# A gated MLP's projection down as Strassen's seven products over pairs of tiles, on one Trainium2 core

## The chip, the cores and the metric

The kernel runs on one core of one Trainium2 chip. The core has a matrix engine (PE, TensorE), a vector engine (DVE), an activation engine (ACT), a general engine (POOL, GpSimd) and a sequencer that mostly issues transfers (SP). Each engine works through its own list of instructions strictly in that list's order, and waits on semaphores where it needs another engine's result. Times are device microseconds (us) of one execution.

## The reference, cut to what matters

One layer of a decoder over 1024 tokens of width 1024: three groups of attention heads, an output projection, a gated MLP of width 2816, a gated per-layer embedding and a last norm. All of it is float32.

```
r  = x + mix @ w_out                                  # 1024 x 1024 @ 1024 x 1024
h2 = rmsnorm(r, ffn_norm)
g  = causal_dwconv3(h2 @ w_gate) + conv_b             # D_FF = 2816
r  = r + (gelu(g) * (h2 @ w_up)) @ w_down             # 2816 -> 1024: the part that is changed
gate = sigmoid(rmsnorm(r, ple_norm) @ w_ple_gate)
r  = r + (p @ w_ple_proj) * gate
return rmsnorm(r, final_norm)
```

## The kernel before, in words

Everything is kept transposed: features on the 128 partitions, tokens along the row. P is 128, T is 1024 (all tokens), H2 is 512 (half of them), KD is 8 tiles of width, NF is 22 tiles of the MLP's width. PE's accumulators are eight PSUM banks of 128 x 512: three under `pg`, five under `b1`.

A float32 product is made of three matmuls (`mm3`, lines 115 to 119): each operand is split by `hl` (line 771) into a rounded part `hi` (a cast on ACT, L772) and the rest `lo` (a subtraction on DVE, L773), and PE adds hi*hi, hi*lo and lo*hi into one bank.

The stages after attention, in program order:

- **Projection out** (`out_tile_half`, line 806): 16 pieces of work, one for each of 8 output tiles and 2 halves of the tokens. Each takes 24 matmuls, its own weights (`wr_wo` from SP's queue, cast to `wh_wo` on ACT, and `wl_wo` by DVE at L106), and ends with the residual's addition on DVE (L813), a write of the half tile to `r_dram` (`rd`) from POOL's queue, and a square on ACT that POOL, or DVE for the last two tiles, adds to `acc2`.
- **Forms and embedding's product** (`form`, `first_halves`): the normed activations and their Strassen combinations are split. The per-layer embedding's product goes to `pp_dram` (`ppd`).
- **Units** (`Unit`, line 907): one for each of the 22 tiles of the MLP's width; it already makes the products with w_gate and w_up by Strassen's seven, 84 matmuls in all, then the convolution and GELU, and multiplies into `us`, which POOL writes to `h3_dram` (line 988). The weights' combinations are made in `weights_up_2`.
- **Projection down**: eight outputs of 128 x 512 at a time, in two passes over f. `h3` comes back from memory, is split again by `h3_parts`, the weights by `weights_down`. The first pass makes output tiles 0 to 3 (both halves), the second tiles 4 to 7, the last seven tiles of f of the second pass output tile by output tile. 8 x 2 x 22 products of three matmuls each. `add_in` adds each to the residual, and `split3` prepares the next product's operand.
- **Embedding's gate** (`embed`): product with w_ple_gate in three pieces of tokens (512, 256, 256), the norm's factor (`rms_bc`), sigmoid, the last norm and the output.

The order on each engine is not the program's order: a scheduler orders all instructions ahead of time by a model of their cost, and `tc.high_priority(offset=...)` moves the instructions in it ahead. A buffer is a slot of a pool under a tag; a tile that takes a slot waits for the last reader of the tile before it. So a tag's number of slots (`BUFS`) sets how far a load may run ahead.

## Time and profile before

| what | us |
|---|---|
| median of 3 runs (lowest to highest) | 1286.43 (1286.18 to 1290.48) |
| the profiled execution, and its span | 1285.93, 1283.7 |
| PE busy, share of the span | 1260.7, 98% |
| DVE, ACT, POOL busy | 815.8 (64%), 537.8 (42%), 103.6 (8%) |
| projection out | about 384 to 450 of the span |
| units 0 to 21 | about 529 to 932 |
| projection down | 932.4 to 1172 |

The profiled execution lies 0.5 us below the median, and 2.2 us of it lie outside the span. The clock granted to PE is full except in the last slice. Windows in the tables of the prediction are in us from the span's start; "L773" is line 773 of the kernel before. In groups of instructions the number behind `x` is their count, then busy time and the mean duration in ns, then the idle time of the engine before them with what ended it.

### The profile page before, as it was taken

Reading aid. Unit: us, or ns where it says so; the run is one execution under the profiler, and the core shown is the slowest. Engines: PE = TensorE matmul, PEld = TensorE weight load, DVE = VectorE, ACT = ScalarE, POOL = GpSimd, SP = SyncE. Lnnn points to the kernel's source line nnn. Section 1 sums busy time; section 2 is a strip of 40 time slices with the busy share of each in tenths; the row PEclk is TensorE's granted clock in tenths of the full one; section 3 lists DMA queues with packets and bytes.
Section 4 is the critical chain, followed back from the end, with each engine's and each line's share of the span. In section 5 each row is a group of like instructions: output and inputs, shape, how many; then the busy total and the mean of one; then the engine's idle time right before and its main releaser. Section 6 shows DMA issues by size and latency. Waiting matters only on the chain.

```text
span 1283.7 us, 16183 instructions
## 1 busy us (share of the span) xinstructions
PE 1260.7 (98%) x6330; PEld 1057.6 (82%) x6330; DVE 815.8 (64%) x1388; ACT 537.8 (42%) x842; POOL 103.6 (8%) x113
## 2 busy tenths in 40 slices
PE   9999999999999999999999999999999999999996
PEld 7888888887888888787888888888888888888896
DVE  7986967567776477976776666666356123346576
ACT  6324233257665256543444344344235123334432
POOL 2000000013111231000000000000000021001010
PEclk9999999999999999999999999999999999999998
DMA  7110110111004745132122222222457215323132
GB/s 250 50 34 17 34 33 18 48 35 34 18 17 143 288 133 197 61 115 99 66 82 99 72 87 88 83 82 77 161 166 262 65 54 200 107 91 115 42 107 82
DMA packets 42236, 122.29 MB, mean 95 GB/s; under 512 B 5168, under 2 KB 7728, under 8 KB 42160
## 3 DMA queue, kind: packets, MB, share of 16 engines
q1 hardware_dynamic: 32032, 89.14, 21.5%
q0 software_dynamic: 8544, 30.41, 6.4%
q10 hardware_dynamic: 1584, 1.71, 0.4%
q8 instruction: 49, 0.80, 0.2%
q14 instruction: 27, 0.22, 0.1%
HBM read 97.13 MB, written 24.12 MB: 94 GB/s over the span
## 4 chain that ended last, share of the span: by engine, by line
PE 68%; issue 11%; DVE 2%; POOL 2%; ACT 1%; DMA 0%; DVEq 0%; POOLq 0%; ACTq 0%
PE d L119 6%; PE d L117 6%; PE d L118 6%; PE gb L119 5%; PE gb L118 5%; PE gb L117 5%; PE gd L117 2%; PE gd L119 2%; PE gd L118 2%; PE pg L118 2%; PE pg L117 2%; PE pg L119 2%; PE o L117 2%; PE o L119 2%; PE o L118 2%
## 5 line engine op out<-in xcount | busy, mean ns | idle before, releaser
L117 PE MATMUL gb<-b,f 128*128 128x512 f32 x176 | 69.1, 393 | 0.2
L118 PE MATMUL gb<-b,f 128*128 128x512 f32 x176 | 68.7, 390 | 0.0
L119 PE MATMUL gb<-b,f 128*128 128x512 f32 x176 | 68.6, 390 | 0.0
L117 PE MATMUL pg<-hp,hpg 128*128 128x256 f32 (+1 forms) x192 | 61.7, 322 | 0.0
L118 PE MATMUL pg<-lp,hpg 128*128 128x256 f32 (+1 forms) x192 | 61.1, 319 | 0.0
L119 PE MATMUL pg<-hp,lpg 128*128 128x256 f32 (+1 forms) x192 | 61.1, 319 | 0.0
L773 DVE TENSOR_TENSOR l<-h3r,h 128x1024 fp32r<-128x1024 f32 x32 | 38.9, 1224 | 34.4 <-ACT h L772 34.2
L976 DVE TENSOR_TENSOR gs<-ga,s 128x512 f32<-128x512 f32 x19 | 13.1, 691 | 68.8 <-PE ga L119 68.8
L772 ACT CAST h<-h3r 128x1024 fp32r<-128x1024 f32 x34 | 35.4, 1050 | 43.2 <-PE d L118 20.2
L988 POOL DMA_DIRECT2D h3d<-us x22 | 11.7, 534 | 415.8 <-DVE us L987 379.9
L781 POOL TENSOR_TENSOR acc<-acc,sq 128x512 f32<-128x512 f32 (+1 forms) x15 | 29.0, 1936 | 166.2 <-ACT sq L780 165.9
L117 PEld LDWEIGHTS gb<-b,f 128*128 128x128 f32 x176 | 33.0, 188 | 8.6 <-ACT gs L939 1.6
L772 ACT CAST f<-s 128x1024 fp32r<-128x1024 f32 x22 | 23.2, 1055 | 38.6 <-PE gb L119 33.7
L119 PEld LDWEIGHTS gb<-b,f 128*128 128x128 f32 x176 | 33.1, 188 | 7.0
L950 ACT ACTIVATE cv<-cv 128x1024 f32<-128x1024 f32 x22 | 23.4, 1061 | 36.7 <-DVE cv L948 36.7
L118 PEld LDWEIGHTS pg<-lp,hpg 128*128 128x128 f32 x192 | 36.6, 191 | 2.6 <-DVE lp L1085 0.2
L119 PEld LDWEIGHTS pg<-hp,lpg 128*128 128x128 f32 x192 | 36.6, 191 | 2.5
L117 PEld LDWEIGHTS pg<-hp,hpg 128*128 128x128 f32 x192 | 36.6, 191 | 2.5
L118 PEld LDWEIGHTS gb<-b,f 128*128 128x128 f32 x176 | 33.1, 188 | 6.7
L772 ACT CAST hf<-s 128x1024 fp32r<-128x1024 f32 x22 | 23.2, 1053 | 31.7 <-PE gd L118 30.5
L119 PE MATMUL gd<-b,f 128*128 128x512 f32 x88 | 34.4, 391 | 1.6 <-DVE f L773 1.6
L773 DVE TENSOR_TENSOR f<-s,f 128x1024 fp32r<-128x1024 f32 x22 | 26.9, 1225 | 14.2 <-ACT f L772 14.2
(781 smaller groups left out, 3942.8 us busy)
## 6 DMA issues: line engine op xcount, KB each, us to landing
wu<-w_gu SPq DMA_DIRECT2D x22, 512.0 KB, 3.5
wg<-w_gu SPq DMA_DIRECT2D x22, 512.0 KB, 3.5
h3d<-us POOLq DMA_DIRECT2D x22, 512.0 KB, 2.9
h3r<-h3d SPq DMA_DIRECT2D x22, 512.0 KB, 3.7
wr_wo<-w_out SPq DMA_DIRECT2D x16, 512.0 KB, 3.6
h3r<-h3d POOLq DMA_DIRECT2D x12, 512.0 KB, 4.0
x<-xT SPq DMA_DIRECT2D x16, 256.0 KB, 5.2
r<-xT SPq DMA_DIRECT2D x16, 256.0 KB, 7.0
```

The costliest lines, as they stand in the source:

```text
L117: TE.matmul(o, wh, xh, start=first, stop=False, skip_group_check=on)
L118: TE.matmul(o, wh, xl, start=False, stop=False, skip_group_check=on)
L119: TE.matmul(o, wl, xh, start=False, stop=last, skip_group_check=on)
L772: S.copy(hi, src)
L773: e.tensor_tensor(out=lo, in0=src, in1=hi.bitcast(F32), op=ALU.subtract)
L781: e.tensor_tensor(out=acc[:, cols], in0=acc[:, cols], in1=sq[:, cols], op=ALU.add)
L950: S.activation(cv, cv, AF.Gelu_apprx_tanh)
L976: V.tensor_tensor(out=g0, in0=bank["a"], in1=s1, op=ALU.add)
L988: G.dma_start(h3_dram[f], us)
```

## The change

`w_down` is taken as 11 pairs of tiles by two blocks of 512 columns: four blocks for each pair. With the activations' two tiles of the pair and two token halves this is a 2 x 2 by 2 x 2 product, made by seven products instead of eight. Each product (1, 2, 6, 5, 7, 3, 4 in this order) runs over all 11 pairs and four output tiles at once: 7 x 11 steps of 4 x 3 matmuls. Four banks ("x") hold a sum that goes on through products 1, 6, 7, 4, four others ("y") product 2, and then 5 and 3. After each product DVE adds the four banks into one half of four residual tiles, 28 additions.

- **The sums of activations.** An even unit writes only half its result (`he_dram`). An odd unit writes its own (`ho_dram`), makes four differences of 128 x 512 on DVE, into `cv` and into the even unit's tile, and writes both (`ta_dram`, `tb_dram`).
- **The sums of weights.** `sums_down(n)`, 22 pieces: POOL's queue loads 512 KB of w_down into the one slot of tag `rs`, DVE makes four sums of 128 x 256 in place, POOL's queue writes 512 KB to `s_dram`. Pieces are put into the program from unit 3 on, one for each unit; nothing but the one slot holds them back.
- **The loads.** `parts(g)` takes two steps at a time: the weights into `wraw` or a slot of `ws`, the activations of four steps into a slot of `hx`, all from SP's queue; then both are split, the activations into `big`.
- **What ends a product.** `done(d, h)` squares a finished half tile of the residual (ACT), adds the square to `acc3` (DVE), and makes the next product's operand (`hp` on ACT, `lp` on DVE). It is called for four tiles after each of the products 2, 7, 3 and 4.
- `weights_up_2` makes its combinations with other operands in place, with as many instructions; tag `ws` has 3 slots instead of 4 and `us` has 2.
- The norm's factor in `embed` is made for the two halves apart.

```diff
+NJ = NF // 2
+DOWN = (1, 2, 6, 5, 7, 3, 4)
...
-    BUFS = {"hx": 6, "r": 8, "gs": 1, "cv": 1, "us": 1, "w4": 1, "w5": 1, "ws": 4}
+    BUFS = {"hx": 6, "r": 8, "gs": 1, "cv": 1, "us": 2, "w4": 1, "w5": 1, "ws": 3}
...
-    h3_dram = [dp.tile([P, T], F32, name=f"h3d{f}") for f in range(NF)]
+    he_dram = [dp.tile([P, H2], F32, name=f"hed{j}") for j in range(NJ)]
+    ho_dram = [dp.tile([P, T], F32, name=f"hod{j}") for j in range(NJ)]
+    ta_dram = [dp.tile([P, T], F32, name=f"tad{j}") for j in range(NJ)]
+    tb_dram = [dp.tile([P, T], F32, name=f"tbd{j}") for j in range(NJ)]
+    s_dram = [dp.tile([4, P, H2], F32, name=f"sd{j}") for j in range(NJ)]
...
-            G.dma_start(h3_dram[f], us)
+            j = f // 2
+            if f % 2 == 0:
+                G.dma_start(he_dram[j], u1)
+                even.append(us)
+                return
+            G.dma_start(ho_dram[j], us)
+            e0, e1 = [even[j][:, half(i)] for i in range(2)]
+            t1, t2 = [cv[:, half(i)] for i in range(2)]
+            minus(t1, e0, e1)
+            minus(t2, u0, t1)
+            G.dma_start(ta_dram[j], cv)
+            minus(e0, u0, e0)
+            minus(e1, u1, t2)
+            G.dma_start(tb_dram[j], even[j])
+    def sums_down(n):
+        j, c = n // 2, slice(n % 2 * 256, n % 2 * 256 + 256)
+        t = cp.tile([P, 4, 256], F32, tag="rs", bufs=1, name=f"sd{n}")
+        G.dma_start(t, a["w_dn"][j][:, :, c].rearrange("b p c -> p b c"))
+        a11, a12, a21, a22 = [t[:, i, :] for i in range(4)]
+        V.tensor_tensor(out=a22, in0=a21, in1=a22, op=ALU.add)
+        minus(a21, a11, a21)
+        minus(a11, a22, a11)
+        minus(a12, a12, a11)
+        G.dma_start(s_dram[j][:, :, c].rearrange("b p c -> p b c"), t)
...
+        sums_down(f - 3)
...
+    for n in range(NF - 3, NF):
+        sums_down(n)
+    steps = [(i, j) for i in DOWN for j in range(NJ)]
+    raws = {}
+    def operands(i, j):
+        w = a["w_dn"][j]
+        x = {1: w[0], 2: w[1], 4: w[3], 6: s_dram[j][0], 3: s_dram[j][1], 7: s_dram[j][2], 5: s_dram[j][3]}[i]
+        y = {1: he_dram[j], 2: ho_dram[j][:, half(1)], 3: ho_dram[j][:, half(0)], 5: ta_dram[j][:, half(0)],
+             6: ta_dram[j][:, half(1)], 7: tb_dram[j][:, half(0)], 4: tb_dram[j][:, half(1)]}[i]
+        return x, y
+    def parts(g):
+        with tc.high_priority(offset=300):
+            if g % 2 == 0:
+                raws[g // 2] = f4("hx", f"hr{g}", (P, 4, H2))
+                for x in range(4 * (g // 2), min(len(steps), 4 * (g // 2) + 4)):
+                    nc.sync.dma_start(raws[g // 2][:, x % 4, :], operands(*steps[x])[1])
+            n = min(2, len(steps) - 2 * g)
+            rw = f4("ws" if g % 2 else "wraw", f"wdr{g}", (P, 2, H2))
+            for x in range(n):
+                nc.sync.dma_start(rw[:, x, :], operands(*steps[2 * g + x])[0])
+            got = []
+            for raw, tags in ((rw, ("whi", "wlo")), (raws[g // 2][:, g % 2 * 2:g % 2 * 2 + 2, :], ("big", "big"))):
+                hi, lo = [f4(t, f"{c}{t}d{g}", (P, 2, H2), F32R) for c, t in zip("hl", tags)]
+                hl(hi[:, :n], lo[:, :n], raw[:, :n])
+                got.append((hi, lo))
+        return got
...
+    def done(d, h):
+        c = half(h)
+        if not acc3:
             acc3.append(f4("ws", "acc3"))
-        sum_squares(acc3[0], r[d], d == 0, tag="ws", e=G if d < KD - 2 else V)
-    def split3(d, tags):
-        hi, lo = [f4(t, f"{c}p{d}", dt=F32R) for t, c in zip(tags, "hl")]
-        for c in [half(0), half(1)] if d == KD - 1 else [slice(0, T)]:
-            S.mul(hi[:, c], r[d][:, c], col(C_G3 + d))
-            V.scalar_tensor_tensor(out=lo[:, c], in0=r[d][:, c], scalar=col(C_G3 + d), in1=hi[:, c].bitcast(F32),
-                                   op0=ALU.mult, op1=ALU.subtract)
-        gs3[d] = (hi, lo)
+        if d == (0 if h else 4):
+            S.square(acc3[0][:, c], r[d][:, c])
+        else:
+            sq = fp.tile([P, H2], F32, tag="s1", bufs=1, name=f"sq{d}{h}")
+            S.square(sq, r[d][:, c])
+            V.tensor_tensor(out=acc3[0][:, c], in0=acc3[0][:, c], in1=sq, op=ALU.add)
+        if d not in gs3:
+            gs3[d] = [f4(t, f"{c}p{d}", dt=F32R) for t, c in zip(TAGS3[d], "hl")]
+        hi, lo = gs3[d]
+        S.mul(hi[:, c], r[d][:, c], col(C_G3 + d))
+        V.scalar_tensor_tensor(out=lo[:, c], in0=r[d][:, c], scalar=col(C_G3 + d), in1=hi[:, c].bitcast(F32),
+                               op0=ALU.mult, op1=ALU.subtract)
...
-        with tc.high_priority(offset=500):
-            raw = f4("ws" if d < 3 or d % 2 else "wraw", f"wpg{d}")
+        with tc.high_priority(offset=300 if d > 2 else 0):
+            raw = f4("us" if d < 3 else "ws" if d % 2 else "wraw", f"wpg{d}")
...
-    for f in range(NF):
-        x = streamed(f, 0) if f < NR else kept(f)
-        h3[f] = x
-        w = weights_down(a["w_dn0"][f], 4, f"a{f}")
-        if f == NF - 4:
-            for i in range(2):
-                residual(i)
+    TO = {1: (0, 1), 6: (0, 0), 7: (4, 0), 4: (4, 1), 2: (0, 1), 5: (4, 0), 3: (0, 0)}
+    DONE = {2: (0, 1), 7: (4, 0), 3: (0, 0), 4: (4, 1)}
+    got = {}
+    bank = {}
+    for n, (i, j) in enumerate(steps):
+        if n % 2 == 0:
+            got[n // 2] = parts(n // 2)
+        if n == 4:
+            for x in range(4):
+                residual(x)
+        (wh, wl), (xh, xl) = got[n // 2]
+        to = "y" if i in (2, 5, 3) else "x"
+        new = i in (1, 2, 5)
+        if new and j == 0:
+            bank[to] = [(pg if (d < 2 if to == "y" else d == 0) else b1)(f"d{i}{d}") for d in range(4)]
         for d in range(4):
-            for h in range(2):
-                down(os[d][h], w, d, x, h, f == 0, f == NF - 1)
-    for d in range(4):
-        add_in(d, os[d])
-    os = banks(1)
-    for n, f in enumerate([*range(NR, NR + NE), *range(NR)]):
-        x = streamed(f, 1) if f < NR else h3[f]
-        w = weights_down(a["w_dn1"][f], 4, f"b{f}")
-        for d in range(4):
-            for h in range(2):
-                down(os[d][h], w, d, x, h, n == 0, False)
-    for d in range(4):
-        split3(d, ("r", "r"))
-    for i in range(2, 4):
-        residual(i)
-    for d in range(4):
-        w = weights_down(a["w_dn2"][d], NK, f"c{d}")
-        for x in (d,) if d < 3 else range(3, KD):
-            gate_weights(x)
-        for h in range(2):
-            for i in range(NK):
-                down(os[d][h], w, i, h3[NR + NE + i], h, False, i == NK - 1)
-        add_in(4 + d, os[d])
-        split3(4 + d, (("gs", "cv"), ("us", "w4"), ("w5", "ws"), ("big", "big"))[d])
+            mm3(bank[to][d], wh[:, n % 2, d * P:d * P + P], wl[:, n % 2, d * P:d * P + P], xh[:, n % 2, :],
+                xl[:, n % 2, :], new and j == 0, j == NJ - 1, not new)
+        if j == NJ - 1:
+            d0, h = TO[i]
+            for d in range(4):
+                V.tensor_tensor(out=r[d0 + d][:, half(h)], in0=bank[to][d], in1=r[d0 + d][:, half(h)], op=ALU.add)
+            if i in DONE:
+                d0, h = DONE[i]
+                for d in range(4):
+                    done(d0 + d, h)
+            if i in (2, 6, 5):
+                gate_weights((2, 6, 5).index(i))
+    for d in range(3, KD):
+        gate_weights(d)
...
-                rms_bc(acc3[0], rs3, slice(0, T), "p")
+                rms_bc(acc3[0], rs3, half(0), "p0")
                 acc4.append(f4("ws", "acc4"))
+            if n == 0 and d == 4:
+                rms_bc(acc3[0], rs3, half(1), "p1")
```

The changed kernel's lines 115 to 117 are `mm3`'s matmuls, 770 and 771 `hl`, 104 the `wl_wo` subtraction, 817 the addition in the projection out, 818 its write `rd`, 1009 and 1015 the load and the write of `sums_down`, 1011 and 878 its sums, 1111 to 1120 `done`, 1156 the additions to the residual.

How the instructions stand on three places. First, DVE in the projection out, before: `wl_wo30` is the `lo` part of the weights for output tile 3, half 0; `r3` the addition of tile 3.

```order
L106 TENSOR_TENSOR wl_wo40_3701<-wr_wo40_3697,wh_wo40_3699 128x1024
L813 TENSOR_TENSOR r2_3545<-o20_3630,r2_3545 128x512
L813 TENSOR_TENSOR r3_3546<-o30_3667,r3_3546 128x512
L106 TENSOR_TENSOR wl_wo50_3738<-wr_wo50_3734,wh_wo50_3736 128x1024
L813 TENSOR_TENSOR r4_3547<-o40_3704,r4_3547 128x512
L106 TENSOR_TENSOR wl_wo60_3775<-wr_wo60_3771,wh_wo60_3773 128x1024
L813 TENSOR_TENSOR r5_3548<-o50_3741,r5_3548 128x512
L106 TENSOR_TENSOR wl_wo70_3812<-wr_wo70_3808,wh_wo70_3810 128x1024
```

The same stretch of DVE in the change; `sd2` is the slot with piece 2 of the weights' sums.

```order
L104 TENSOR_TENSOR wl_wo40_3734<-wr_wo40_3730,wh_wo40_3732 128x1024
L1011 TENSOR_TENSOR sd2_5185<-sd2_5185 128x256
L878 TENSOR_TENSOR sd2_5185<-sd2_5185 128x256
L817 TENSOR_TENSOR r2_3578<-o20_3663,r2_3578 128x512
L878 TENSOR_TENSOR sd2_5185<-sd2_5185 128x256 x2
L817 TENSOR_TENSOR r3_3579<-o30_3700,r3_3579 128x512
L104 TENSOR_TENSOR wl_wo50_3771<-wr_wo50_3767,wh_wo50_3769 128x1024
L817 TENSOR_TENSOR r4_3580<-o40_3737,r4_3580 128x512
L1011 TENSOR_TENSOR sd3_5325<-sd3_5325 128x256
L104 TENSOR_TENSOR wl_wo60_3808<-wr_wo60_3804,wh_wo60_3806 128x1024
L878 TENSOR_TENSOR sd3_5325<-sd3_5325 128x256 x3
```

Pieces 0 to 5 stand on DVE between the weights' splits of the projection out, from piece 2 on one for every two output tiles, and pieces 6 and 7 among its last tiles; POOL's list has each piece's load and write between the `rd` writes and the additions to `acc2`. From unit 0 to unit 8 the other pieces follow, three for every two units.

Second, ACT where product 2 ends and product 6 begins, in the change. PE goes from product 2's last matmul straight to one that reads `hwhid11`, the `hi` weights of group 11 (two steps, the first two of product 6); the fourth matmul reads their `lo`, which DVE makes from it. `rr0` and `rr1` are residual tiles, `hpg1` a part of w_ple_gate.

```order
L1111 ACTIVATE acc3_7958<-rr0_7610 128x512
L1119 ACTIVATE hp0_7960<-rr0_7610,small_68 128x512
L1114 ACTIVATE sq11_7964<-rr0_7610 128x512
L1119 ACTIVATE hp1_7967<-rr0_7610,small_68 128x512
L770 CAST hpg1_8210<-wpg1_8208 128x1024
L1119 ACTIVATE hp2_7974<-rr1_7613,small_68 128x512
L770 CAST hwhid11_7994<-wdr11_7991 128x1024
```

The cast of the weights for the next product stands behind six instructions of `done` and `gate_weights`, the first of which needs product 2's first finished bank.

Third, ACT where product 7 ends and product 3 begins. Group 28, whose activations are `hbigd28`, begins with product 3's second step, 12 matmuls after product 7's last; its third matmul reads the `lo` part of those activations.

```order
L770 CAST hwhid28_8688<-wdr28_8685 128x1024
L1111 ACTIVATE acc3_7958<-rr2_7616 128x512
L1119 ACTIVATE hp4_8643<-rr2_7616,small_68 128x512
L1114 ACTIVATE sq50_8647<-rr2_7616 128x512
L1119 ACTIVATE hp5_8650<-rr2_7616,small_68 128x512
L1119 ACTIVATE hp6_8657<-rr3_7619,small_68 128x512
L1119 ACTIVATE hp7_8664<-rr3_7619,small_68 128x512
L770 CAST hwhid29_8723<-wdr29_8720 128x1024
L1114 ACTIVATE sq60_8654<-rr3_7619 128x512
L770 CAST hbigd28_8692<-hr28_8680 128x1024
```

Here it is the activations' cast that stands behind `done` of product 7.

More of the change, by code (lines that the diff above doesn't have):

```diff
@@ L1046, in down @@
-    def down(o, w, i, x, h, first, last):
-        mm3(o, w[0][:, i, :], w[1][:, i, :], x[0][:, half(h)], x[1][:, half(h)], first, last)
-    def streamed(f, again):
-        return h3_parts(f, again, *[f4("r", f"{c}3{f}{again}", dt=F32R) for c in "hl"])
-    def kept(f):
-        if f == NF - 1 or f == NF - 2:
-            t = f4("hx", f"h3{f}", (P, 2, T), F32R)
-            return h3_parts(f, 0, t[:, 0], t[:, 1])
-        return h3_parts(f, 0, *[f4("big", f"{c}3{f}", dt=F32R) for c in "hl"])
@@ L1058, in banks @@
-    def banks(p):
-        return [[(pg if d * 2 + h < 3 else b1)(f"d{p}{d}{h}") for h in range(2)] for d in range(4)]
+    for n in range(NF - 3, NF):
[8 more added lines that the diff above has]
+        return x, y
```

48 lines of the change are left out of this document (12 added, 36 removed).

## The prediction

> **What bounds the kernel now.** First the page: how full each engine is, slice by slice, and the chain that ended last.
>
> ```profile
> PE 1260.7 (98%) x6330; PEld 1057.6 (82%) x6330; DVE 815.8 (64%) x1388; ACT 537.8 (42%) x842; POOL 103.6 (8%) x113
> DVE  7986967567776477976776666666356123346576
> PE 68%; issue 11%; DVE 2%; POOL 2%; ACT 1%; DMA 0%; DVEq 0%; POOLq 0%; ACTq 0%
> ```
>
> PE is full from end to end and is the chain. So a matmul taken away is worth its place in PE's stream, as long as nothing new makes PE wait. Where DVE is at eight or nine tenths, added DVE work has little room. Second, busy time by stage (the windows of the trace; PE's count is that of its matmuls).
>
> ```profile
> core 0: us, PE busy (x) PEld busy (x) DVE busy (x) ACT busy (x) POOL busy (x), PEclk, DMA share, GB/s
> ...
> 404.00:436.00 32.00, 32.00 (x143) 26.30 (x142) 13.68 (x15) 11.12 (x14) 11.70 (x12) 1.00 0.93 350
> ...
> 529.00:568.00 39.00, 37.07 (x160) 29.27 (x159) 32.82 (x42) 19.35 (x22) 0.97 (x2) 1.00 0.31 104
> 604.00:924.00 320.00, 319.47 (x1407) 263.70 (x1407) 204.31 (x244) 130.04 (x152) 9.05 (x17) 1.00 0.27 90
> 932.40:1172.00 239.60, 239.60 (x1056) 197.74 (x1055) 98.66 (x103) 77.32 (x91) 19.24 (x18) 1.00 0.42 134
> ```
>
> The last row is the projection down: PE busy for all of 239.60 us with 1056 matmuls, 239.60 / 1056 = 0.227 us for each. DVE is at 98.66 / 239.60 = 41% there and the transfers at 134 GB/s; nothing but PE's count sets that stage. The first row is the stage that matters for the added transfers: the DMA engines are 93% busy through the middle of the projection out, at 350 GB/s.
>
> **The matmuls that go.** 16 output halves x 22 tiles x 3 = 1056 become 7 products x 11 pairs x 4 outputs x 3 = 924, of the same shape. 132 x 0.227 = **-29.9 us**. The stage keeps pace otherwise: a group of two steps is 24 matmuls, 5.44 us, and needs two casts and two subtractions of 128x1024.
>
> ```profile
> L773 DVE TENSOR_TENSOR l<-h3r,h 128x1024 fp32r<-128x1024 f32 x32 | 38.9, 1224 | 34.4 <-ACT h L772 34.2
> L772 ACT CAST h<-h3r 128x1024 fp32r<-128x1024 f32 x34 | 35.4, 1050 | 43.2 <-PE d L118 20.2
> ...
> L1076 DVE TENSOR_TENSOR rr<-d,rr 128x512 f32<-128x512 f32 x16 | 10.6, 687 | 11.3 <-PE d L119 11.3
> L1155 ACT ACTIVATE rr<-rr,small 128x512 f32<-128x512 f32 x8 | 5.8, 724 | 2.4 <-DVE pt L1153 2.2
> L780 ACT ACTIVATE sq<-rr 128x512 f32<-128x512 f32 x6 | 3.8, 629 | 7.5 <-DVE rr L1149 7.5
> ```
>
> That is 2.1 us of ACT and 2.4 us of DVE in 5.44, and 1 MB of loads, 193 GB/s against the 350 just seen. With two `whi` slots the cast waits for the group before last to end and is done about 2.5 us later (cast, then subtraction, with hand-overs), 2.9 us early. This cover holds in the middle of a product.
>
> **Two boundaries where it doesn't.** ACT's list puts the work of `done` ahead of the cast that the next product needs. Count from the end of product 2's last matmul. Its first bank is complete nine matmuls earlier, at -2.0; DVE adds it in 0.69, from -1.8 with the hand-over to -1.1. Then ACT does, in order, a square (0.63), a scaled copy (0.72), a square, a scaled copy, the cast of a gate weight (1.05) and a scaled copy: 0.63 + 0.72 + 0.63 + 0.72 + 1.05 + 0.72 = 4.5, to +3.4. Only then comes the cast of group 11's weights, to +4.4, and DVE's `lo` part, to +5.6 or 5.7. PE starts at +4.4, has three matmuls (0.7), and waits again until 5.7: a stall of **5.0 us**. Where product 7 ends, ACT has one square, then 0.72 + 0.63 + 3 x 0.72, the weights' cast 1.05, another square, and then the activations' cast: -1.1 + 0.63 + 0.72 + 0.63 + 2.16 + 1.05 + 0.63 + 1.05 = +5.8, and DVE's `lo` at +7.3 behind a norm addition and `lp7`. PE has the second half of a group to do until 2.72, and two matmuls of the next: 7.3 - 2.72 - 0.45 = **4.2 us**. Sum 9.2, from 7 (hand-overs shorter) to 11. The other three changes of product have the next operands cast ahead in the lists: 0.
>
> **The sums of weights in the projection out.** A piece is load, four DVE sums, write, and then the next load into the one slot: a closed loop. DVE waits for each load in its list, with the weights' splits for PE behind it; whoever is late makes `wl_wo` late, and PE waits for that. The list gives a loop two output tiles, 2 x 24 x 0.227 = 10.9 us. The loop's parts, from the nearest rows (transfers with KB each and us from issue to landing; the first `rd` row is of the window 404 to 436, the second of 450 to 560):
>
> ```profile
> rd<-r POOLq DMA_DIRECT2D x7, 256.0 KB, 5.7
> ...
> ppd<-pst POOLq DMA_DIRECT2D x8, 512.0 KB, 4.4
> ...
> rd<-r POOLq DMA_DIRECT2D x7, 256.0 KB, 2.3
> ...
> ppt<-ppd POOLq DMA_DIRECT2D x4, 512.0 KB, 4.1
> ...
> L620 DVE TENSOR_TENSOR pT<-tb,tmask 128x256 f32<-128x256 f32 x3 | 1.3, 421 | 2.0 <-ACT pT L619 2.0
> ```
>
> Without other load: 4 x 0.42 = 1.7, write 4.4, load 4.1, hand-overs 0.5: 10.7, just the room there is. Between 404 and 436 the same write of 256 KB takes 5.7 instead of 2.3, 3.4 more. With 3.4 more on each transfer the loop is 17.5, 6.6 more than its room. DVE has some room of its own there:
>
> ```profile
> 422.58 0.69 DVE L813 TENSOR_TENSOR r<-o,r 128x512 f32<-128x512 f32 x1 [3.31 <-PE o L119]
> 428.02 0.69 DVE L813 TENSOR_TENSOR r<-o,r 128x512 f32<-128x512 f32 x1 [3.31 <-PE o L119]
> ```
>
> It idles 3.3 us for each tile. So the first slow loop costs 6.6 - 3.3 = 3.3, the next, with the cover gone, up to 6.6; the stretch holds two loops of 17.5, and lateness pushes the third out of it. 3.3 + 4.7 (between the covered and the full price, nearer the full, since POOL's list also has additions to `acc2` between write and load) = **8 us**; from 2 (the load stays at 4 us) to 20 (three loops, none covered).
>
> [...]
>
> **The sums beside the units.** A unit is 84 matmuls, 19.04 us. DVE has 204.31 / 320 x 19.04 = 12.2 of it. Three pieces for two units add 2.6 to each, and the four differences of an odd unit:
>
> ```profile
> L874 DVE TENSOR_TENSOR s<-wg,wu 128x512 f32<-128x512 f32 x15 | 10.3, 685 | 0.0
> ```
>
> 4 x 0.69 = 2.7. An odd unit has 17.5 of 19.04: hidden behind PE. The loop has 38.1 / 3 = 12.7 us there, against 10.7. Only at the start is DVE short: 32.82 of 39 between 529 and 568, plus three pieces (5.0) and one set of differences (2.7), 40.5 of 39. **2 us**, from 0 to 14 (three loops at 17.5 instead of 12.7).
>
> **The end.** After product 4 DVE's list has, ahead of the broadcast of the norm's factor for the first half of the tokens, four additions, four norm additions, four `lp` (near 0.75 each), three subtractions of gate weights and twelve small steps, one every 0.2:
>
> ```profile
> 1275.07 0.17 DVE rq_t L142
> 1275.27 0.17 DVE rb_yf L143
> ```
>
> 8 x 0.69 + 4 x 0.75 + 3 x 1.22 + 12 x 0.2 = 14.6, begun at -1.8: 12.8, with hand-overs about 13.5. PE comes to the broadcast after 56 matmuls, at 12.7: **0.8 us**, from 0 to 3.
>
> **Sum.** -29.9 + 9.2 + 8 + 2 + 0.8 = -9.9. The profiled execution took 1285.93 (span 1283.7, 2.2 outside): 1276.0; the median of the runs is 0.5 higher: **1276.5 us**.
>
> **Rivals.**
> - **The sums are hidden everywhere.** The loads land in 4 us although the DMA engines are full, because the rest of that traffic is early loads for later tiles. -29.9 + 9.2 + 0.8: 1266.5. For it: no wait of PE on a transfer between 404 and 436. Against it: the 5.7 us.
> - **The loop eats the gain.** 16 in the projection out and 5 at the start: -29.9 + 9.2 + 16 + 5 + 0.8 = +1.1, 1287.5. For it: DVE can't pass a waiting sum, POOL's additions stand between write and load. Against it: the burst ends at 436.
> - **Slower: the loop sets the pace of the units.** It decides from 12.7 us on: rows of 1 KB, 512 of them, where `ppd` has 256, could make the loop 14, and 13 pieces would lose 1.3 each, 17. With 16 in the projection out: -29.9 + 9.2 + 16 + 17 + 0.8 = +13, 1299.5. Against it: the DMA engines are at 27% in the units, about half with the new traffic.
> - **The clock falls in the stalls.** PE's longest wait is 2.5 us, and only the end shows what follows idle time:
>
> ```profile
> PE rb_f L166 <- DVE rb_yf L143: 2.5, 1, 2.5
> ...
> 1264.00:1270.00 6.00, 6.00 (x53) 6.00 (x52) 3.48 (x9) 2.90 (x8) 0.00 (x0) 1.00 0.00 0
> 1276.00:1283.00 7.00, 1.19 (x4) 0.93 (x4) 2.50 (x5) 0.00 (x0) 0.00 (x0) 0.50 0.45 150
> ...
> 1256.17 0.64 PE rb_f L166 x4
> 1276.16 1.21 PE rb_f L166 x4
> ```
>
> The same four matmuls take 1.21 us instead of 0.64 after some 6 us with PE mostly idle, at half the clock. If PE ran at half clock for as long as it had stood, 5.0 and 4.2 us of stall would cost 4.6 more: 1281. [...] The drop agrees with the trace; how long it lasts no row shows.
>
> **How the numbers follow.** Forecast 0.46 (its own range 1270 to 1283), hidden 0.17, gain eaten 0.20, slower 0.12, clock 0.05. A measurement tells 0.5% from no change: below 1280.0 is faster, above 1292.9 slower. Faster: 0.37 of the forecast, 0.16 of hidden, 0.01 of the clock: 0.54. Slower: 0.11 of the slow rival, 0.04 of the eaten gain, 0.01 of the forecast: 0.16. The rest, 0.30, is the same. The range goes from a little under the hidden case, 1264, into the gap before the slow one, 1294.
>
> **What would show it.** The down stage should be about 209.5 + 9 us, with 924 matmuls and two PE waits of 4 to 5 us, on ACT's weight cast and DVE's activation `lo`. Between 400 and 450 PE should wait for `wl_wo`, with DVE idle ahead of a sum of `sd` until a transfer lands. Odd units should take 19.0 us. I am wrong if PE waits inside a product, if the `sd` transfers take over 6 us in the units, or if PE doesn't wait in the projection out at all.

## The result, and the profile after

The change makes the kernel slower: 1306.49 us (1305.42 to 1310.03) against 1286.31 us (1285.46 to 1290.48), a ratio of 1.0155 with a 95% interval of 1.0126 to 1.0184. The prediction said 1276.5. The profiled execution is the longest of the runs, 1310.03, 3.5 above the median, so its span, 24.6 us longer than that of before, shows about four microseconds more than the runs do. How much of that lies in which stage is not known; in e4 below, whose program is the same up to the projection down, the first row of the table is 18.2 instead of 20.8.

First the page of the changed kernel, with the same rows as before:

```profile
PE 1249.9 (96%) x6198; PEld 1041.7 (80%) x6198; DVE 907.7 (69%) x1567; ACT 553.1 (42%) x860; POOL 128.1 (10%) x162
PE   9999999999999789999999999999999899899996
PEclk9999999999999889999999999999999899899998
```

PE does 132 matmuls less and is yet at 96% of a longer span. Three notches stand in its row, a wide one and two narrow ones, and each has its notch in the row of the granted clock: slices 14 and 15 of the 40 (the projection out), and two near the end (the projection down).

The stages are measured by the start of the last matmul of each. In the names, `h` and `l` stand for `hi` and `lo`: `hwhid` and `lwlod` are the two parts of the weights of the projection down, `hbigd` and `lbigd` those of its activations. These rows list the matmuls of a tile, with their count, duration in ns (lowest, median, highest), and the start of the first and the last of them; the first four are of the kernel before, from four answers of the trace,

```profile
L119 PE MATMUL o<-hc,wl_wo x32: 388/389/390, 402.6 to 483.9; 128*128 128x512 f32 x32
...
L119 PE MATMUL pp<-pT,wl_pp x32: 389/389/476, 484.6 to 508.0; 128*128 128x512 f32 x32
...
L119 PE MATMUL gb<-b,f x176: 387/389/398, 534.6 to 932.2; 128*128 128x512 f32 x176
...
L119 PE MATMUL d<-h,wdc3wlo x14: 389/389/390, 1163.3 to 1172.1; 128*128 128x512 f32 x14
```

and these of the change:

```profile
L117 PE MATMUL o<-hc,wl_wo x32: 388/389/395, 403.1 to 504.7; 128*128 128x512 f32 x32
...
L117 PE MATMUL pp<-pT,wl_pp x32: 389/389/628, 505.4 to 531.4; 128*128 128x512 f32 x32
...
L117 PE MATMUL gb<-b,lf x176: 387/389/628, 563.0 to 972.1; 128*128 128x512 f32 x176
...
L117 PE MATMUL d<-hbigd,lwlod x308: 387/389/642, 972.8 to 1197.1; 128*128 128x512 f32 x154
```

| us | before | change | difference |
|---|---|---|---|
| to the end of the projection out | 483.9 | 504.7 | +20.8 |
| embedding's product | 24.1 | 26.7 | +2.6 |
| units | 424.2 | 440.7 | +16.5 |
| projection down | 239.9 | 225.0 | -14.9 |
| the rest of the span | 111.6 | 111.2 | -0.4 |

The projection down saves half of what its matmuls are worth; the three stages ahead of it, whose matmuls the change doesn't touch, lose 39.9.

What PE waited for in the change (the trace's waits of PE: total, times, longest; a choice of rows, those of the projection down all among them):

```profile
PE o L117 <- DVE wl_wo L104: 8.1, 2, 6.5
PE gb L115 <- DVE us L944: 4.8, 5, 1.9
PE rb_r L164 <- DVE rb_yr L141: 4.7, 1, 4.7
PE d L115 <- ACT hwhid L770: 4.2, 2, 3.6
PE gd L115 <- ACT us L941: 3.4, 2, 1.8
PE d L115 <- ACT hbigd L770: 2.7, 1, 2.7
...
PE d L116 <- DVE lbigd L771: 1.2, 1, 1.2
...
PE d L117 <- DVE lwlod L771: 0.7, 1, 0.7
```

The rows of `d` are the projection down's, 4.2 + 2.7 + 1.2 + 0.7 = 8.8. Not all of it stands at the two boundaries that the prediction names. The timeline has four of the five waits here (start, duration, what ran; in brackets the idle time before, and what ended it):

```profile
989.31 0.50 PE L115 MATMUL d<-hbigd,hwhid 128*128 128x512 f32 x1 [0.52 <-ACT hwhid L770]
...
990.76 0.50 PE L117 MATMUL d<-hbigd,lwlod 128*128 128x512 f32 x1 [0.72 <-DVE lwlod L771]
...
1136.09 1.22 PE L115 MATMUL d<-hbigd,hwhid 128*128 128x512 f32 x2 [2.66 <-ACT hbigd L770]
1138.50 0.79 PE L116 MATMUL d<-lbigd,hwhid 128*128 128x512 f32 x1 [1.19 <-DVE lbigd L771]
```

The last two are where product 7 ends; the wait where product 2 ends, 3.65, is shown under e4. So the boundaries have 3.65 + 2.66 + 1.19 = 7.5, and 1.2 stand inside product 1, soon after the stage begins.

Behind `wl_wo` and `rb_yr` stands DVE in the projection out. Its timeline there:

```profile
419.54 0.42 DVE L1011 TENSOR_TENSOR sd<-sd 128x256 f32<-128x256 f32 x1 [4.51 <-DMA sd<-w_dn]
...
424.60 0.69 DVE L817 TENSOR_TENSOR r<-o,r 128x512 f32<-128x512 f32 x1 [0.29 <-PE o L117]
435.31 0.42 DVE L1011 TENSOR_TENSOR sd<-sd 128x256 f32<-128x256 f32 x1 [10.02 <-DMA sd<-w_dn]
435.65 1.22 DVE L104 TENSOR_TENSOR wl_wo<-wr_wo,wh_wo 128x1024 fp32r<-128x1024 f32 x1
...
451.07 0.43 DVE L1011 TENSOR_TENSOR sd<-sd 128x256 f32<-128x256 f32 x1 [5.22 <-DMA sd<-w_dn]
451.41 1.22 DVE L104 TENSOR_TENSOR wl_wo<-wr_wo,wh_wo 128x1024 fp32r<-128x1024 f32 x1
```

DVE idles 10.02 us until the load of a piece lands, and the next thing in its list, the moment after the first sum, is the weights' split for which PE stands still. From piece to piece it takes 15.8 us (419.54, 435.31, 451.07), where the list has two output tiles, 10.9. The clock falls with these stalls, at 430.06 and 463.98 us, of 6.47 and 4.65 (windows with PE's busy time and count of matmuls in front; the third number from the end is the granted clock):

```profile
432.90:443.10 10.20, 6.18 (x15) 4.83 (x16) 4.48 (x7) 0.63 (x1) 2.60 (x3) 0.50 0.59 200
467.10:473.80 6.70, 4.78 (x15) 4.19 (x16) 6.03 (x17) 2.44 (x4) 3.44 (x4) 0.50 0.84 273
```

### The profile page after: what moved, and what is told of

It is laid out like the page before. It is cut to its first block, busy times and chain, and to the rows that moved or that the text cites. A ratio compares the mean times of both kernels' runs of the same rounds, so it can differ in the third digit from the quotient of the medians.

```text
span 1308.3 us, 16434 instructions
## 1 busy us (share of the span) xinstructions
PE 1249.9 (96%) x6198; PEld 1041.7 (80%) x6198; DVE 907.7 (69%) x1567; ACT 553.1 (42%) x860; POOL 128.1 (10%) x162
## 5 line engine op out<-in xcount | busy, mean ns | idle before, releaser
L115 PE MATMUL d<-hbigd,hwhid 128*128 128x512 f32 x308 | 122.2, 398 | 6.8 <-ACT hwhid L770 4.2
L116 PE MATMUL d<-lbigd,hwhid 128*128 128x512 f32 x308 | 122.1, 397 | 1.2 <-DVE lbigd L771 1.2
L117 PE MATMUL d<-hbigd,lwlod 128*128 128x512 f32 x308 | 121.8, 395 | 0.7 <-DVE lwlod L771 0.7
L771 DVE TENSOR_TENSOR lwlod<-wdr,hwhid 128x1024 fp32r<-128x1024 f32 (+1 forms) x39 | 47.0, 1208 | 70.8 <-ACT hwhid L770 70.7
L115 PE MATMUL gb<-b,hf 128*128 128x512 f32 x176 | 70.2, 399 | 6.5 <-DVE us L944 4.8
L115 PEld LDWEIGHTS d<-hbigd,hwhid 128*128 128x128 f32 x308 | 59.0, 192 | 20.5 <-ACT hwhid L770 5.0
L115 PE MATMUL gd<-b,f 128*128 128x512 f32 x176 | 68.9, 392 | 3.5 <-ACT us L941 3.4
L116 PEld LDWEIGHTS d<-lbigd,hwhid 128*128 128x128 f32 x308 | 59.1, 192 | 14.2 <-DVE lbigd L771 1.9
L117 PEld LDWEIGHTS d<-hbigd,lwlod 128*128 128x128 f32 x308 | 59.1, 192 | 13.7 <-DVE lwlod L771 1.5
L117 PE MATMUL gd<-b,f 128*128 128x512 f32 x176 | 68.3, 390 | 1.5 <-DVE f L771 1.5
L116 PE MATMUL gb<-b,hf 128*128 128x512 f32 x176 | 69.3, 394 | 0.0
L117 PE MATMUL gb<-b,lf 128*128 128x512 f32 x176 | 69.3, 394 | 0.0
L116 PE MATMUL gd<-b,f 128*128 128x512 f32 x176 | 68.5, 389 | 0.0
L770 ACT CAST hbigd<-hr 128x1024 fp32r<-128x1024 f32 (+1 forms) x39 | 40.3, 1038 | 16.3 <-DMA hr<-hod 8.9
```

Source lines behind the costliest of these rows:

```text
L115: TE.matmul(o, wh, xh, start=first, stop=False, skip_group_check=on)
L116: TE.matmul(o, wh, xl, start=False, stop=False, skip_group_check=on)
L117: TE.matmul(o, wl, xh, start=False, stop=last, skip_group_check=on)
L770: S.copy(hi, src)
L771: e.tensor_tensor(out=lo, in0=src, in1=hi.bitcast(F32), op=ALU.subtract)
```

## The experiments

The theory (W in the expectations): DVE, which can't pass an instruction in its list, stands behind the loads of the weights' pieces, and what PE needs stands behind it. Its rivals: DVE has too much to do beside the units (F), and the added transfers themselves slow the others (T). In the table, times of a stage are worked out as above; the expectations reckon the projection out by another of its rows, 1.4 us earlier. Kernels with a single run (e1 to e6, e8, e10, e12, e13) have no interval; the kernel before took 1286.6 to 1288.0 in the sets of runs beside them.

| kernel | time | to the end of the projection out | embedding's product | units | down |
|---|---|---|---|---|---|
| before | 1286.3 | 483.9 | 24.1 | 424.2 | 239.9 |
| the change | 1306.5 | 504.7 | 26.7 | 440.7 | 225.0 |
| e1, no sums of weights | 1273.9 | 485.6 | 24.1 | 427.8 | 223.0 |
| e2, their transfers alone | 1315.7 | 513.0 | 38.2 | 428.9 | 222.7 |
| e3, pieces from unit 3 on | 1289.3 | 484.1 | 24.1 | 446.2 | 221.7 |
| e4, slots given early | 1292.1 | 502.1 | 26.4 | 440.6 | 209.6 |
| e5, e3 with sums on POOL | 1358.4 | 484.1 | 24.1 | 515.0 | 222.2 |
| e6, their DVE work alone | 1273.4 | 484.0 | 24.1 | 428.5 | 222.9 |
| e7, e5 with e4 | 1348.2 | 485.6 | 24.1 | 517.2 | 210.5 |
| e8, e3 with e4 | 1279.7 | 485.7 | 24.2 | 446.9 | 209.4 |
| e9, one piece a unit, e4 | 1279.4 | 486.2 | 24.1 | 432.9 | 223.5 |
| e10, e3 with added writes | 1289.5 | 484.2 | 24.1 | 446.1 | 222.0 |
| e11, e9 spread otherwise | 1278.6 | 485.7 | 24.1 | 446.9 | 209.5 |
| e12, e1 with e4 | 1257.1 | 484.2 | 24.1 | 425.6 | 210.0 |
| e13, e6 with added writes | 1278.3 | 485.7 | 24.1 | 432.1 | 223.1 |
| e14, pieces at the end of units, e4 | 1262.0 | 484.0 | 24.1 | 430.8 | 211.3 |

**e1: the sums of weights left out.** `sums_down` returns at once, and `operands` reads `w[0]` to `w[3]` in place of `s_dram`.

> All weight sums are left out: no piece is loaded, summed or written, and the four products that would read them read blocks of w_down instead (same sizes, other values). The activations' differences stay. In the change's trace the projection out took 20.9 us longer than before (last matmul at 503.4 instead of 482.5), the embedding's product 2.5, the units 16.5, the projection down 225.1 instead of 239.9. Theory W (DVE stands in its list behind a piece's load) and rival T (the added transfers slow the others): the projection out is back at 86 us, the units within 3 us of 421; 1306.5 - 21 - 2.5 - 14 = 1269, between 1264 and 1274. Rival F (DVE is too full in the units, with the activations' differences as a part): the units keep 5 or more, 1274 to 1280.

1273.9. The loss of the projection out goes but for 1.7, and 12.9 of the units' 16.5 belong to the pieces. The time lies where the ranges of W and T and of F meet, and the 3.6 that stays in the units lies between their marks, so e1 doesn't part the theories. The 3.6 stands at the units' start, a wait of 2.4 us on ACT's `whig` among it; in e12, the same kernel up to there, 1.4 stays, with a wait of 1.8: no matmul of its `ga` and `gb` takes over 504 ns, where e1 has some of 628 and a granted clock of 0.97 between 515 and 575. Between 575 and 935 us PE was busy for 359.9 of 360, so the activations' differences cost nothing there.

**e2: the transfers without the sums.**

```diff
-        a11, a12, a21, a22 = [t[:, i, :] for i in range(4)]
-        V.tensor_tensor(out=a22, in0=a21, in1=a22, op=ALU.add)
-        minus(a21, a11, a21)
-        minus(a11, a22, a11)
-        minus(a12, a12, a11)
```

> The loads and writes of all 22 pieces stay, with their one slot; only the four DVE sums of each piece are left out, so DVE never waits for a piece (the values written are the blocks themselves). Theory W and rival F: as without the pieces, 1266 to 1274, though the transfers are the same 22 MB. Rival T (transfers slow the others): near the change, 1296 or more, with the projection out 15 us longer than before.

1315.7, slower than the change: theory W's number is missed by 40 us. But the trace doesn't say T either. These are the waits between 384 and 510, of POOL, and what follows from them:

```profile
POOL sd L1010 <- DMA sd<-w_dn: 46.0, 12, 8.0
POOL sd L1009 <- DMA sd<-sd: 40.3, 11, 5.2
ACT sq L778 <- POOL acc L779: 34.7, 6, 14.5
DVE wl_wo L104 <- ACT wh_wo L102: 20.4, 9, 13.0
```

Without sums the loop runs on POOL alone, whose next load waits for the write and whose next write waits for the load, 86 us of waits. Behind them in POOL's list stand the additions to `acc2`, behind these ACT's squares, behind these the weights' cast. The standing moved from DVE to POOL, and with it the stall. Theory W had to be worded anew: not DVE, but whichever engine has the wait in its list. Units of 428.9 say nothing for or against T here, since the write of the 17th of the 22 pieces is issued at 555.27 us and the units run from 551 to 980.

**e3: no piece before unit 3.**

```diff
+        if f == 3:
+            hold = cp.tile([P, 4, 256], F32, tag="rs", bufs=1, name="hold")
+            V.tensor_copy(out=hold[:, 0, :1], in_=even[1][:, :1])
         sums_down(f - 3)
```

> The one slot is held by a one-column copy of unit 2's result, so no piece starts before unit 3; the pieces then follow between units 3 and 18, nothing else is changed. Theory W: the projection out and the embedding's product lose nothing (-23.4), the units lose by the number of pieces among them, 22 instead of 14, so 16.5 x 22 / 14 = 26 instead of 16.5: 1306.5 - 23.4 + 9.5 = 1293, 1287 to 1297, with DVE waits on the pieces' loads in the units. Rival F: the loss in the units was at their start, where DVE is fullest and where now no piece falls: 1306.5 - 23.4 - 10 = 1273. Rival T: 1290 to 1306, since the same transfers are made elsewhere.

1289.3: the projection out and the embedding's product are back at their old times, and the units lose more, 446.2, with 22 pieces instead of 14 among them. That is (446.2 - 427.8) / 22 = 0.84 us for a piece, in the change (440.7 - 427.8) / 14 = 0.92. Rival F's 1273 is off. T's range begins at 1290, so by the time alone T is hardly excluded.

**e4: the slots of `acc3` and the last operand given early.**

```diff
             for x in range(4):
                 residual(x)
+            acc3.append(f4("ws", "acc3"))
+            gs3[7] = [f4("big", f"{c}p7", dt=F32R) for c in "hl"]
+            for x in (acc3[0], *[y.bitcast(F32) for y in gs3[7]]):
+                G.memset(x[:, :1], 0.0)
```

> acc3 and the last operand's two tiles are given their slots at the fifth step of the projection down, by a one-column memset each; ACT's list then has the next product's casts ahead of the work that ends a product. Theory on the boundaries: the two PE stalls there (4.2 and 0.7 us on the weights, 2.7 and 1.2 on the activations, 8.8 in all) go, and with them the time at a lower clock after each, about 4.6: 1306.5 - 13.4 = 1293, projection down 211 to 213 us. Rival (the clock after a stall costs nothing): 1298, 216 us. Rival (PE only waits elsewhere, later in the product): 1304 or more.

1292.1, the projection down 209.6, less than the 211 to 213 expected; PE has no wait in it at all (a window of the stage; PE's busy time and its count of matmuls follow the length):

```profile
969.30:1179.00 209.70, 209.70 (x926) 173.48 (x926) 125.51 (x133) 92.68 (x105) 3.06 (x5) 1.00 0.64 211
```

209.7 us, with 926 matmuls in the window, is 29.9 below the 239.6 of before. The projection down costs 225.0 - 209.6 = 15.4 more in the profiled run of the change, of which 8.8 are waits, 7.5 of them at the boundaries. In the change, at the end of product 2 (matmuls of the same shape, start and duration):

```profile
1033.73 0.39 PE L117 MATMUL d<-hbigd,lwlod 128*128 128x512 f32 x1
1037.77 0.79 PE L115 MATMUL d<-hbigd,hwhid 128*128 128x512 f32 x1 [3.65 <-ACT hwhid L770]
...
1038.79 0.63 PE L115 MATMUL d<-hbigd,hwhid 128*128 128x512 f32 x1
1039.22 0.64 PE L117 MATMUL d<-hbigd,lwlod 128*128 128x512 f32 x1
...
1043.91 0.39 PE L117 MATMUL d<-hbigd,lwlod 128*128 128x512 f32 x1
1044.14 0.40 PE L115 MATMUL d<-hbigd,hwhid 128*128 128x512 f32 x1
```

After an idle 3.65 us matmuls start every 0.43 us instead of 0.23, until 1043.91, for 6.1 us. The granted clock at the two boundaries:

```profile
1037.06:1043.89 6.83, 6.12 (x14) 4.63 (x15) 5.61 (x7) 3.38 (x5) 0.00 (x0) 0.50 0.49 150
...
1136.06:1142.87 6.81, 5.59 (x12) 3.97 (x13) 6.39 (x7) 3.46 (x4) 0.00 (x0) 0.50 0.43 138
```

It is half for 6.8 us both times. The 14 matmuls of the first stretch take 6.1 us where 3.2 is their time at 0.227 each, the 12 of the second 5.6 where it is 2.7: 5.8 lost to the clock. Waits of 8.8 and a clock of 5.8 leave 0.8 of the 15.4 open. Less idle is enough ahead of the second stretch: after 2.66 us the next two matmuls already take 1.22, and only then PE waits 1.19 more.

**e5 and e6** part W from F in the units. e5 is e3 with the four sums as POOL's instructions; e6 has the four DVE instructions alone, on one resident tile, the first reading a column block of the unit before:

```diff
+        a11, a12, a21, a22 = [res[0][:, i, :] for i in range(4)]
+        V.tensor_tensor(out=a22, in0=a21, in1=u[:, :256], op=ALU.add)
```

> As e3 (pieces from unit 3 on), but the four sums of a piece are made by POOL instead of DVE; the transfers and their slot stay, everything is computed. e3 took 1289.3 us with 446.2 us from the embedding's product to the last unit's end; without weight sums (e1) that stretch took 427.8. Theory W (DVE stands behind a late load): POOL stands behind it instead, where only the units' writes are queued; the stretch falls to 428 to 432, time 1271 to 1276. Rival F (DVE too full): the same, since DVE's work goes too; the two part with the next kernel. Rival T (transfers slow the weights' loads): the stretch stays at 440 or more, 1284 or more. A loss is possible where POOL's and DVE's instructions lengthen each other (POOL's additions took 1.3 us with an idle DVE and up to 2.6 beside a busy one).

> The four DVE instructions of each of the 22 pieces without its transfers: they work on one resident tile, three pieces for every two units from unit 3 to 17, each tied to the unit before by one operand; the products read blocks of w_down, so the weights' sums are left out of the result. Theory W: DVE has the same work as in e3 and no load to stand behind, so the stretch from the embedding's product to the last unit takes 428 to 432 us and the time is 1274 to 1278, as without any sums. Rival F: the stretch takes 440 to 446, 1286 to 1290.

e6: 1273.4, units 428.5, PE busy without a gap though DVE is at 259.54 / 320 = 81% (604 to 924):

```profile
604.00:924.00 320.00, 320.00 (x1410) 264.28 (x1410) 259.54 (x366) 128.65 (x154) 19.29 (x36) 1.00 0.33 112
```

F falls: DVE has room for all of it. e5: 1358.4, missed by over 80 us. The longest waits of the units there, of ACT and POOL:

```profile
ACT us L941 <- DMA hod<-us: 85.8, 7, 17.6
...
POOL sd L1014 <- DMA sd<-w_dn: 75.2, 22, 5.4
...
POOL sd L1012 <- DMA sd<-sd: 61.7, 20, 4.6
```

POOL stands behind its pieces for 137 us. The expectation took it that only the units' writes are queued there, as if they could wait. They can't: `hod` is late, so `us` comes free late, so ACT's copy of the next unit into it waits 85.8 us, and PE's banks with it. **e7** is the same with e4's slots:

> e5 and e4 together, complete: pieces from unit 3 on, their sums on POOL, slots of acc3 and the last operand's tiles given early. If the losses add up as separate terms: e5's time less 13 to 15 (what e4 took off: 1306.5 to 1292.1), 1257 to 1263, ratio to before 0.977 to 0.982. If POOL and DVE lengthen each other: 1265 to 1275.

1348.2, a ratio of 1.0462 (1.0444 to 1.0481), some 85 us above the range. Only e4's part of the expectation held, 210.5 in the projection down.

**e8: e3 and e4 together.**

> e3 and e4 together, sums still on DVE. Adding the two savings: 1306.5 - 17.2 - 14.4 = 1275, 1272 to 1278. It prices what is left of DVE's standing in the units (against e7) with both other losses gone.

1279.7. The units are at 446.9 and the projection down at 209.4, so the two losses are separate. It came 2 us above the range given: the two savings, taken from single times, add up to 31.6 and gave 26.8.

**e9: at most one piece a unit.** The slot is held before each piece by a one-column copy from the unit before; three pieces are left for the end.

```diff
+        if after is not None:
+            hold = cp.tile([P, 4, 256], F32, tag="rs", bufs=1, name=f"hold{n}")
+            V.tensor_copy(out=hold[:, 0, :1], in_=after[:, :1])
...
-        sums_down(f - 3)
+        sums_down(f - 3, last_us[f - 1])
```

> e8 with one piece for each unit from unit 3 on (the slot is held by a one-column copy of the unit before; the last three follow at once): everything is computed, sums on DVE, slots given early. Theory W, that DVE loses by standing behind loads that land later than the list allows: in e8 three pieces in two units left a loop 12.7 us for some 11 to 12; now a loop has 19 us, and what DVE waits for a late landing (1 to 2 us once in a unit) is inside its 3.5 us of room in a unit. The stretch from the embedding's product to the last unit falls from 446.9 (e8) to 428 to 433, time 1262 to 1268, ratio 0.981 to 0.985. Rival (each piece costs its 0.9 us of PE wherever it stands): 22 x 0.85 = 18.7 stays, 1279.

Units 432.9, as forecast: the rival, a fixed price for each piece, falls, though its number, 1279, is the time that came. 1279.4 came since the projection down took 223.5, with waits of PE on the first weights, behind DVE waits of up to 9.3 us on the three pieces left (waits between 943 and 1170, PE's, and between 943 and 1000, DVE's):

```profile
PE d L117 <- DVE lwlod L771: 5.4, 4, 2.7
PE d L115 <- ACT hwhid L770: 4.7, 3, 2.1
...
DVE sd L1017 <- DMA sd<-w_dn: 13.4, 3, 9.3
```

The ratio is 0.9945 (0.9933 to 0.9958), the first whose interval lies below 1.

**e10: added writes in the projection out.** Each half tile of the residual is written to memory twice more from POOL's queue.

> e3 with two further copies of every half tile of the residual written to unused memory from POOL's queue in the projection out: 8 MB of added transfers there, as much as the change's pieces move in that stage or more, with nothing that waits for them. Theory W: the projection out ends within 3 us of e3's (482.7), 1287 to 1293. Rival T (the added traffic itself, by late weights or residual loads, stalls PE there): it ends 8 us or more later, 1297 or more.

1289.5, and the projection out ends at 484.2. The transfers did get slower (window 404 to 436): the residual's loads took 10.3 us instead of the 7.0 of before. PE lost nothing by it. T falls for this stage.

```profile
r<-xT SPq DMA_DIRECT2D x16, 256.0 KB, 10.3
...
jk<-r POOLq DMA_DIRECT2D x14, 256.0 KB, 7.8
```

**e11: e9 with no piece left for the end.** One in each of the units 3 to 20, a second in the units 6, 10, 14 and 18, all with the hold. **e12** is e1 with e4.

> e9 with all 22 pieces done by unit 21: one for each of the units 3 to 20, a second one in four even units, none at the end, so that the projection down starts with nothing of them in DVE's list. In e9 the units took 433 us as forecast (e8: 447), but the last three pieces followed at once after the units and the projection down took 223 instead of 209 (e8), with a DVE wait of 9.3 us on a piece. Theory W: units 430 to 436, projection down 209 to 211, 1264 to 1270, ratio 0.982 to 0.987. Rival (the 13 us in the projection down came from the early slots, not from the last pieces): 1277 or more.

> e1 (weight sums left out, so not the reference's values) with the slots given early: what is left when both the pieces and the two boundaries cost nothing. By the terms as separate: e1's 1273.9 less 12 to 15 (e3 to e8: 9.7, the change to e4: 14.4), 1259 to 1264; the matmuls' 29.9 alone would give 1256.5, and 3.6 us of that e1 loses at the start of the units.

e11: 1278.6, ratio 0.9933 (0.9919 to 0.9946), 9 us above its range. The projection down is back at 209.5, as W has it. The units aren't: 446.9 instead of 430 to 436. In the units with two pieces two loops share a unit's 19 us, and DVE stands for the load, and at the hold for the write of the piece before (DVE, waits of the units):

```profile
DVE sd L1018 <- DMA sd<-w_dn: 33.7, 14, 5.1
...
DVE hold L1013 <- DMA sd<-sd: 7.1, 7, 1.6
```

41 us of standing, against 25.3 in e3 and 12.0 in e9's units. That e11's units take no longer than e3's with so much more of it is not explained. e12: 1257.1, 2 us below its range: without pieces and boundaries the change is worth 29.6 (1286.8 beside it, a single run) of the 29.9 that its matmuls promise.

**e13 and e14: transfers without standing, and everything without standing.** e13 adds three writes of 512 KB to each of 16 units of e6. e14 is complete: a piece belongs to a unit, and its sums come after a one-column operation that reads the unit's finished tile. The load follows the write of the piece before and has almost a unit to land.

```diff
+        V.tensor_tensor(out=pin, in0=a22[:, :1], in1=after[:, :1], op=ALU.add)
         V.tensor_tensor(out=a22, in0=a21, in1=a22, op=ALU.add)
...
+            sums_down(f, us)
             j = f // 2
```

> e6 (the pieces' DVE work without their transfers, so not the reference's values) with three further writes of the unit's 512 KB tile to unused memory from POOL's queue in units 3 to 18: 1.5 MB for a unit, as many bytes as three pieces in two units move, and nothing that waits for them but the tile's next use. Theory W: units within 4 us of e6's 428.5, 1272 to 1278. Rival T (it is the transfers themselves that hold up the units, by later loads of weights): units 438 or more, 1283 or more.

> Complete, with the slots given early: one piece for each of the 22 units, its four sums behind a one-column DVE operation that reads the unit's own finished tile. So the sums stand on DVE a whole unit, 19 us, after the write of the piece before; its write and the next load take some 8 to 9. Nothing is held by a wait on a transfer. Same DVE work, same transfers. Theory W: DVE waits for no piece, units 425 to 431, projection down 209, 1257 to 1263, within 4 us of e12 (1257.1, no sums at all); ratio 0.977 to 0.982. Rivals (transfers or DVE's load set the units): units 440 or more, 1270 or more.

e13: 1278.3, just above W's range, units 432.1, 3.6 above e6. The added writes made the units' own longer (`tbd` took 7.0 us from issue to landing between 600 and 900, 3.5 in the change between 604 and 924), more than the pieces do, and left the loads of the units' weights at 3.5; so 3.6 is likely more than what the pieces' transfers cost the units. e14: 1262.0 us (1261.6 to 1264.6), a ratio of 0.9809 (0.9796 to 0.9823). It has the change's work, DVE busy 907.2 us against 907.7, the same 22 MB of pieces, and these are all its DVE waits for pieces:

```profile
DVE pin L1014 <- DMA sd<-w_dn: 1.5, 2, 1.3
```

The time and the units, 430.8, are near the upper ends of their ranges, and the projection down takes 211.3 instead of 209. e14 less e12 is 4.9, where 4 was the most expected: that is about what the sums of weights cost where nobody stands behind them. e14 changes two things at once, the place of the sums and the pace, one piece for each unit. e9 has the pace alone, and already brings the units from 446.9 to 432.9; its last three pieces, which e14 has inside the units, cost it 14 in the projection down.

## Why the prediction was wrong, point by point

**The matmuls.** -29.9 was right: 209.7 us without stalls (e4) against 239.6, and 29.6 of it in the time of e12.

**The two boundaries.** 9.2 was forecast, 7.5 us of waits came, at the places and for the reason named: e4 moves the casts ahead, and they go. Where product 2 ends, one wait of 3.65 came instead of a stall of 5.0 in two pieces; where product 7 ends, 2.66 + 1.19 instead of 4.2 (7.3 - 2.72 - 0.45 is 4.1). But with the clock the boundaries cost 7.5 + 5.8 = 13.3: the step that failed is that a stall was priced by its length. The rival "the clock falls in the stalls" had the mechanism, with 4.6 to be added and 5.8 measured; it was given 0.05 and belonged into the sum. Its premise, half clock for as long as PE had stood, was an estimate: half rate lasted 6.8 us both times, after waits of 3.65 and of 2.66 + 1.19. The other 2.0 of the stage's 15.4 are the 1.2 of waits inside product 1, which the prediction names as a sign of being wrong, and 0.8 that were not pursued.

**The projection out.** 8 was forecast, from 2 to 20, and 20.8 came, and 2.6 more in the embedding's product (18.2 and 2.3 in e4, whose program is the same up to there). The mechanism was right: DVE stood before the sums with the weights' split behind them, and the loops of a piece took 17.5, 15.8, 15.8 and 13.5 us, where 17.5 was worked out. Mis-sized was what covers it. "The stretch holds two loops": DVE waited for five pieces in a row, 4.5, 10.0, 5.2, 5.6 and 3.1 us, since the loops lengthen the stretch. And 13.9 of the 20.8 are waits of PE; some 5.5 of the other 6.9 are the clock, half of the 10.96 us for which PE was busy at 0.50, which was not in this term either.

**The units.** 2 was forecast and 16.5 came, 12.9 of it by the pieces (e1). "The loop has 12.7 us there, against 10.7", so the sums were taken as hidden: this is the step that failed in its reasoning, and not only in a size. On average the loop holds: from 618 to 707 us the loops took 9.8 to 14.8, 12.7 in the mean. It is no average that counts. Each sum has a place in DVE's list, and a load that lands a few us after that place makes DVE stand, whatever room follows: 16.3 us in the change, 25.3 in e3, 1.5 in e14, none in e6, which has the sums without the loads. A second path stands beside it: in the change ACT waits 15.1 us for the units' own writes `hod`, which are in POOL's list with the pieces, and 3.4 us of PE's waits are for the `us` that ACT then makes (none in the units of e1, 1.1 in e14); how much of the loss is this path's is not shown. That the pieces would be too much for DVE at the start was the wrong worry: the 3.6 that stays there in e1 comes without any piece, and PE's wait on `whig` is 2.5 in the change and 2.4 in e1.

No single term turned the sign. Without the miss in the units, 14.5, the kernel would still be 5.7 slower than before by the runs' 20.2, and without that of the projection out and the embedding's product, 15.4, 4.8 slower.

**The rivals.** The slower one (a chance of 0.12, 1299.5) came nearest: 16 in the projection out and 17 in the units were 20.8 and 16.5. Its number for the units is luck: the reason given, rows of 1 KB that make the loop 14, is not what the traces show. Loads and writes of a piece took 4.3 and 3.8 us, as the rows for 512 KB had them, and the loop didn't need to be longer on average to cost 12.9. "Hidden everywhere" is refuted by e3 and the DVE waits: its loads of 4 us took 8.4 in the change between 404 and 436.

**The end.** 0.8 was forecast, -0.4 came.

## What to carry to other kernels

Before a closed loop of transfers (load, work, write, load) is put beside a full engine, ask in whose list its waits stand and what stands behind them; bytes and busy shares of this change fit well, and moving the waits from DVE to POOL (e2, e5) made it worse. Give each piece a whole period, here 19 us, and place the consumer late by a true dependence on work that is late anyway (e14). Holding the load back alone does it where a piece has a period to itself (the units of e9), and not where two share one (e11). And a stall of PE is priced with what its clock takes afterwards: here 7.5 us of waits at the boundaries brought 5.8 more, with a single idle of 2.66 us already enough.

## What the runs showed that was not expected

The same sums and transfers took 1262 us (e14), 1280 (e8) and, with the sums on POOL, 1348 (e7), by the place of their waits. A one-column memset that gives a tile its slot early (e4) is worth 14 us, since ACT's list then has the next product's casts ahead of the work that ends a product. It is not the loads that were late: in the change those of product 6's first weights are issued at 1025.39, and ACT casts them from 1036.69 on. POOL's sums lengthened DVE beside them: in e5's units the subtraction `lf` of 128x1024 took 1437 ns in the mean of 15 between 560 and 920, against 1218 in the mean of 19 there in the change.
